# Score products of a two-layer diffusion trunk: two float32r products per head and block from stacked high and low parts

## The chip, the cores and the metric

The kernel runs on one core of a Trainium2 chip. The metric is the device time of one execution in microseconds, the median of several runs. A core has TensorE (matrix products), VectorE, ScalarE and GpSimd, which run side by side, each in the order of its own queue, and SyncE, which here only issues DMAs.

## The reference, cut to what matters

A trunk of two layers handles 128 prompt tokens and 256 sample tokens of width 1024. Each layer is a feed-forward part, a mixer and a second feed-forward part. The mixer of layer 0 (the even one) is a linear recurrence beside a differential attention; the mixer of layer 1 (the odd one) is a windowed attention with grouped queries. The sample tokens also see 128 cached keys.

```python
def diff_attn_block(qb, k, v, lam):              # even: 4 heads, each with 2 halves m of width 64
    s = jnp.einsum('bqhmd,bthmd->bhmqt', qb, k)
    p = jax.nn.softmax(s, axis=-1)
    w = p[:, :, 0] - lam * p[:, :, 1]
    return jnp.einsum('bhqt,bthe->bqhe', w, v)

def gqa_sink_block(qb, k, v, mask, sink):        # odd: 16 query heads of width 64 on 4 key heads
    s = jnp.einsum('bqkgd,btkd->bkgqt', qb, k)
    ...
```

Before these products queries and keys are normalized and, for the sample tokens, rotated. Everything is float32.

## The kernel before, in words

All data lie transposed: features on the 128 partitions (rows of a tile), the 384 tokens on the columns, 128 of the prompt and then 256 of the sample.

Weights come in chunks of 1 MB on SyncE's queue. Each group of eight 128x128 weights is split into a high part (a float32r copy, on ScalarE or VectorE) and a low part (a subtraction on VectorE), three groups ahead of their use. A weight product is then three float32r products (`mm3`): high with high, high with low, low with high.

The order of the work is made while the program is written. One main stream issues TensorE's projections (`proj_pass`, `out_pass`) and feed-forward products. All else runs as chains, Python generators that yield what they wait for. After each product `tick` looks at a list of chains and emits the stage whose inputs, by a table of estimated times, should be there. The recurrence of the even mixer (`lru_tile`) yields `DVE_IDLE` and `ACT_IDLE`: it is emitted where the engine is estimated to have nothing queued. The helper `copy` chooses between ScalarE and VectorE by the same estimates and takes VectorE only if that is done 0.5 us earlier. The estimates order the program and are not measurements.

In the even mixer the projection tiles are four for the recurrence, then query, key and value of each of four heads, then four gate tiles; then the output projection starts, with the K tiles of the four heads first and those of the recurrence last. In the odd mixer a key tile, a value tile and four query tiles come twice; each query tile holds two heads. There is no filler work in the odd mixer.

A query tile goes through `q_chain`: out of PSUM, norm, gain, a DMA that swaps the two rows of a rotary pair, two products and an add. A key tile goes through `k_chain`. A tile holds two score halves, rows 0 to 63 and 64 to 127, and the scores of each are needed alone. So `k_chain` writes each half into a tile of its own, `kz[0]` and `kz[1]`, whose other 64 rows GpSimd sets to zero, and beside it come the cached keys, stored with zeros in the same way. A product of the whole query tile with `kz[m]` then gives half m alone.

`scores` issues the products of one block: 128 queries (block 0 is the prompt, blocks 1 and 2 the sample) against 128 or 384 keys, for both m. In the even mixer a sample block is two fp32 products. In the odd mixer (`split=True`) query and keys are first split into high and low, and a sample block is six float32r products, three for each m, and then two mask products in bfloat16 (`identb`, `trib`). The prompt block is two fp32 products of 128 columns in both. The next step of a block (`a_chain`) is the softmax on VectorE and ScalarE, four or six transposes on TensorE, and `o_chain` applies the weights to the values.

PSUM has two banks for projections (`mm`), two pairs for scores (`sc`), which the feed-forward part uses too, and two for the rest (`ms`).

Of the kernel before, what the change touches and what calls it, by code (L numbers as in the profile page):

```python
# [15 lines left out]
ALU = mybir.AluOpType  # L16
# [13 lines left out]
RANGES = ((slice(0, NP_), 0), (slice(NP_, T), 1))  # L30
N_SLAB = 79
# [16 lines left out]
class Event:  # L48
    """Something that a chain of instructions has still to emit, with the tiles that it leaves."""
# [5 lines left out]
class Banks:  # L55
    """PSUM tiles of one tag: how many may be in use at a time, and when the free ones fell free."""
# [5 lines left out]
class Idle:  # L62
    """Ready when an engine has nothing else queued."""
# [19 lines left out]
class Clock:  # L83
    """Rough times of the engines while the program is written: they order the emission and nothing else."""
# [34 lines left out]
class Sched:  # L119
    """Emits the stages of side chains between pieces of the matmul stream, each when its inputs should be there."""  # L120
# [81 lines left out]
class Eng:  # L202
    """An engine's instructions, timed by the clock as they are written."""
# [50 lines left out]
def emit(tc, D, order):  # L254
    nc = tc.nc
    ctx = ExitStack()
    with ctx:
# [64 lines left out]
        def copy(out, in_, scale=None):  # L322
            """out = in_ (times a column), on the engine that should be done with it first."""
            k = {} if scale is None else {"scale": scale}
            r = max(clock.at(in_)[0], clock.at(out)[0])
            ta = max(clock.free["ACT"], r) + S_.cost("activation", out, [in_], k)
            td = max(clock.free["DVE"], r) + V.cost("tensor_copy", out, [in_] if scale is None else [in_, scale], k)
            if td + ON_ACT < ta:
                if scale is None:
                    V.tensor_copy(out, in_)  # L330
                else:
                    V.tensor_scalar(out, in_, scale, None, ALU.mult)
            else:
                act(out, in_, AF.Copy, **k)

# [140 lines left out]
        def mod_one():  # L476
            """Generator: one modulation tile, a condition per stage."""
# [44 lines left out]
        def prep(d, with_sh=True):  # L522
            """Generator: scaled x as two float32r parts, and the sum of squares."""
# [36 lines left out]
        def normed_all(low):  # L560
            """Starts the chains that leave the normed and modulated x as two float32r parts."""
# [152 lines left out]
        def qk_norm(t, bc, gate, gs):  # L714
            """Generator: leaves the normed rows in t, then returns the two parts of the rotated ones."""
# [29 lines left out]
        def q_chain(ps, direct, gate, gs, out):  # L745
            def gen():
# [5 lines left out]
                if not out.get("split"):  # L752
                    V.tensor_tensor(t[:, NP_:T], u[:, 0:NS], a[:, 0:NS], ALU.add)
                    sched.fire(out["q_ev"], t)
                    return
                V.tensor_tensor(u[:, 0:NS], u[:, 0:NS], a[:, 0:NS], ALU.add)
                hi, lo = sl(F32R, NS), sl(F32R, NS)
                yield u
                copy(hi, u[:, 0:NS])
                yield hi  # L760
                V.tensor_tensor(lo, u[:, 0:NS], r32(hi), ALU.subtract)
                out["qs"] = hi, lo
                sched.fire(out["q_ev"], t, hi, lo)
            sched.add(gen())

        def k_chain(ps, direct, gate, gs, out, ctx_src, k_out):
            def gen():
                yield ps
                t, bc = evac(ps, direct)
                kz = [sl(), sl()]  # L770
                kp = sl()
                kpv = kp.rearrange("p (a b) -> p a b", a=3)
                G.memset(kz[0][64:128, NP_:T], 0.0)
                G.memset(kz[1][0:64, NP_:T], 0.0)
                G.memset(kpv[64:128, 0, :], 0.0)
                G.memset(kpv[0:64, 1, :], 0.0)
                for m in range(2):
                    G.dma_start(kz[m][:, 0:NP_], ctx_src[m])
                out["kz"], out["kp"] = kz, kpv
                sched.fire(out["kp_ev"])  # L780
                yield t
                u, a = yield from qk_norm(t, bc, gate, gs["k"])
                for m in range(2):
                    h = slice(64 * m, 64 * m + 64)
                    V.tensor_tensor(kz[m][h, NP_:T], u[h, 0:NS], a[h, 0:NS], ALU.add)
                for m in range(2):
                    h = slice(64 * m, 64 * m + 64)
                    copy(kpv[h, m, :], t[h, 0:NP_])
                    G.dma_start(k_out[h, :], kpv[h, m, :])
                if not out.get("split"):  # L790
                    sched.fire(out["k_ev"], kz[0], kz[1], kp)
                    return
                out["ks"] = []
                for m in range(2):
                    hi, lo = sl(F32R), sl(F32R)
                    out["ks"].append((hi, lo))
                    yield kz[m]
                    copy(hi, kz[m])
                    yield hi
                    V.tensor_tensor(lo, kz[m], r32(hi), ALU.subtract)  # L800
                sched.fire(out["k_ev"], kp, *out["ks"][0], *out["ks"][1])
# [21 lines left out]
        def transposed(src, n):  # L823
            """w (128 queries, n*128 keys) -> SBUF (keys, n, queries)."""
# [8 lines left out]
        def scores(kv, q, qt, more=False):  # L833
            ps = sct()
            n = 1 if qt == 0 else 3
            for m in range(2):
                if qt and "ks" in kv:
                    (qh, ql), (kh, kl) = (v[:, (qt - 1) * P:qt * P] for v in q[1]), kv["ks"][m]
                    mm(ps[:, m, :n * P], qh, kh, True, False)
                    mm(ps[:, m, :n * P], ql, kh, False, False)  # L840
                    mm(ps[:, m, :n * P], qh, kl, False, not more)
                    continue
                rhs = kv["kp"][:, m, :] if qt == 0 else kv["kz"][m]
                mm(ps[:, m, :n * P], q[0][:, qt * P:(qt + 1) * P], rhs, True, not more)
            return ps, n

        def proj_pass(tiles, key, done, low):
            """Projection tiles in order; the first two share a K order that leaves the last tile of x late."""
# [32 lines left out]
        def out_pass(key, gm, nxt, ready, free_at, early, wide):  # L881
            """Output projection. The K tiles in `early` come first: x takes their part while the others are computed."""
# [8 lines left out]
            def slot(t, ps):  # L891
                """A bank that has nothing to do: kept while there are units to come."""
# [69 lines left out]
        def even_mixer(nxt):  # L962
# [136 lines left out]
            def a_chain(h, qt):  # L1099
                H = heads[h]  # L1100
                yield H["k_ev"], H["q_ev"], scb
                ps, n = scores(H, (H["q"], None), qt)
# [69 lines left out]
        def odd_mixer(nxt):  # L1172
# [6 lines left out]
            kvs = [dict(split=True, k_ev=Event(), v_ev=Event(), kp_ev=Event()) for _ in range(2)]  # L1179
            its = [dict(split=True, q_ev=Event(), w={}, w_ev=[Event() for _ in range(3)]) for _ in range(8)]  # L1180
# [69 lines left out]
        def mixer_consts():  # L1250
            yield RS.ev, el, pp
            # differential lambda, negated
# [5 lines left out]
            # -8 * softplus(-lam) on (128, 2 directions, 4 tiles); log1p by its series in z / (2 + z)  # L1258
# [91 lines left out]
# order of the 64 rows of a q or k head on the partitions: the two rows of a rotary pair side by side  # L1350
# [136 lines left out]
```

## Time and profile before

| | |
|---|---|
| median of 3 runs | 1466.14 us (1464.9 to 1466.73) |
| span of the profiled execution | 1464.2 us |
| instructions in the profile | 21823 |
| MB moved by DMA | 250.67 |
| even mixer | about 318 to 482 us of the span |
| odd mixer | about 1041 to 1188 us of the span |

The profiled execution's span runs from its first to its last instruction; it is the time that the profile tells of, and the runs' median lies 1.9 us above it. A busy share is the time in which an engine has at least one instruction in work. Nearly all instructions carry the line of one helper (L214), so groups are told apart by tile names: `sc`, `mm` and `ms` are the PSUM tiles, `s` is any tile of the general pool, `hi` and `lo` are the parts of a weight, `raw` a weight as it is loaded. An fp32 product appears as two records of TensorE, a float32r product as one. PEld is the loading of the stationary operand, which overlaps with products.

### The profile page before, as it was taken

Reading aid. Unit: us, or ns where it says so; the run is one execution under the profiler, and the core shown is the slowest. Engines: PE = TensorE matmul, PEld = TensorE weight load, DVE = VectorE, ACT = ScalarE, POOL = GpSimd, SP = SyncE. Lnnn points to the kernel's source line nnn. Section 1 sums busy time; section 2 is a strip of 40 time slices with the busy share of each in tenths; the row PEclk is TensorE's granted clock in tenths of the full one; section 3 lists DMA queues with packets and bytes.
Section 4 is the critical chain, followed back from the end, with each engine's and each line's share of the span. In section 5 each row is a group of like instructions: output and inputs, shape, how many; then the busy total and the mean of one; then the engine's idle time right before and its main releaser. Section 6 shows DMA issues by size and latency. Waiting matters only on the chain.

```text
span 1464.2 us, 21823 instructions
## 1 busy us (share of the span) xinstructions
PE 1436.7 (98%) x8354; PEld 1398.4 (96%) x8354; DVE 1115.4 (76%) x2103; ACT 659.8 (45%) x1193; POOL 103.8 (7%) x214
## 2 busy tenths in 40 slices
PE   4999999999999999999999999999999999999998
PEld 1999999998889999999999999999998899999998
DVE  3899999969998998999979997444698795444332
ACT  3643333348875633333345333333477664333321
POOL 0001111110220011111100110000100000000000
PEclk9999999999999999999999999999999999999999
DMA  9557767652322366766744766333331233333430
GB/s 361 216 185 257 246 245 257 235 173 101 120 99 97 140 230 236 254 243 231 254 177 153 251 243 196 135 119 130 117 107 51 77 120 115 133 126 116 146 135 22
DMA packets 49560, 250.67 MB, mean 171 GB/s; under 512 B 6464, under 2 KB 10960, under 8 KB 28336
## 3 DMA queue, kind: packets, MB, share of 16 engines
q1 hardware_dynamic: 29664, 180.05, 34.0%
q0 software_dynamic: 19792, 69.23, 14.2%
q8 instruction: 66, 1.08, 0.3%
q14 instruction: 38, 0.31, 0.1%
HBM read 244.53 MB, written 2.36 MB: 169 GB/s over the span
## 4 chain that ended last, share of the span: by engine, by line
PE 95%; DMA 2%; DVE 2%; ACT 1%; issue 0%; SPq 0%; DVEq 0%; ACTq 0%
PE sc L214 54%; PE mm L214 36%; PE ms L214 5%; DVE s L214 1%; DMA wm<-in_wm 1%; DMA s<-in_xT 1%; DMA raw<-in_wst 0%; DVE lo L214 0%; ACT s L214 0%; DMA s<-s 0%; ACT hi L214 0%; ACT L317 0%; SPq L737 0%; SPq L1296 0%; DVEq L1434 0%
## 5 line engine op out<-in xcount | busy, mean ns | idle before, releaser
L214 PE MATMUL sc<-s,hi 128*128 128x384 f32 (+1 forms) x2816 | 726.3, 339 | 2.3 <-ACT s L214 1.4
L214 ACT ACTIVATE hi<-raw 128x1024 fp32r<-128x1024 f32 x298 | 315.7, 1060 | 541.7 <-PE sc L214 307.4
L214 DVE TENSOR_TENSOR lo<-raw,hi 128x1024 fp32r<-128x1024 f32 x312 | 381.3, 1223 | 231.2 <-ACT hi L214 230.0
L214 PE MATMUL mm<-s,hi 128*128 128x384 f32 (+1 forms) x2072 | 545.8, 344 | 2.3 <-DVE s L214 2.3
L214 PEld LDWEIGHTS sc<-s,hi 128*128 128x128 f32 x2816 | 512.6, 188 | 5.0 <-ACT s L214 1.8
L214 PE MATMUL sc<-s,lo 128*128 128x384 f32 (+1 forms) x1408 | 475.4, 338 | 0.0
L214 PEld LDWEIGHTS mm<-s,hi 128*128 128x128 f32 x2072 | 372.9, 188 | 12.4 <-issue 3.0
L214 PE MATMUL mm<-s,lo 128*128 128x384 f32 (+1 forms) x1036 | 349.1, 337 | 0.0
L214 DVE CUSTOM_DVE_ANT_0 junk<-wm,cbc 128x1024 bf16<-128x1024 f32 x256 | 312.6, 1221 | 11.0 <-DMA wm<-in_wmt 8.3
L214 PEld LDWEIGHTS sc<-s,lo 128*128 128x128 f32 x1408 | 265.0, 188 | 0.0
L214 PEld LDWEIGHTS mm<-s,lo 128*128 128x128 f32 x1036 | 194.7, 188 | 0.0
L214 ACT ACTIVATE s<-s 128x384 f32<-128x384 f32 (+3 forms) x215 | 108.0, 507 | 171.9 <-DVE s L214 157.0
L214 DVE TENSOR_TENSOR s<-s,s 128x384 fp32r<-128x384 f32 (+6 forms) x214 | 112.0, 528 | 20.0 <-ACT s L214 18.9
L214 POOL DMA_DIRECT2D wm<-in_wmt x126 | 66.6, 528 | 695.1 <-DVE M L214 674.2
L214 DVE SCALAR_TENSOR_TENSOR s<-s,M,s 128x128 fp32r<-128x128 f32 (+3 forms) x256 | 92.4, 416 | 3.8 <-ACT s L214 3.7
L214 ACT ACTIVATE s<-s,M 128x256 fp32r<-128x256 f32 (+1 forms) x167 | 66.3, 446 | 11.0 <-DVE s L214 8.1
L214 DVE SCALAR_TENSOR_TENSOR s<-mm,M,s 128x128 f32<-128x128 f32 x104 | 38.5, 412 | 32.2 <-PE mm L214 32.2
L214 DVE TENSOR_TENSOR s<-sc,s 128x384 f32<-128x384 f32 x106 | 56.8, 551 | 0.0
L214 PE MATMUL sc<-s,s 128*128 128x384 f32 (+2 forms) x208 | 49.0, 373 | 0.7 <-ACT s L214 0.7
L214 ACT ACTIVATE s<-ms 128x384 f32<-128x384 f32 (+3 forms) x80 | 31.8, 423 | 29.8 <-PE ms L214 29.5
L214 PEld LDWEIGHTS sc<-s,s 128*128 128x128 f32 x208 | 34.1, 189 | 7.0 <-ACT s L214 1.3
L214 ACT ACTIVATE s<-sc,sm 128x385 f32<-128x385 f32 (+3 forms) x72 | 35.9, 511 | 0.0
(107 smaller groups left out, 635.1 us busy)
## 6 DMA issues: line engine op xcount, KB each, us to landing
raw<-in_wst SPq DMA_DIRECT2D x156, 1024.0 KB, 5.0
wm<-in_wmt POOLq DMA_DIRECT2D x126, 512.0 KB, 3.8
wm<-in_wm SPq DMA_DIRECT2D x8, 1024.0 KB, 7.6
s<-s SPq DMA_DIRECT2D x36, 64.0 KB, 2.4
s<-in_xT SPq DMA_DIRECT2D x8, 192.0 KB, 7.4
out_y<-s SPq DMA_DIRECT2D x8, 192.0 KB, 1.9
cbc<-in_c_rows SPq DMA_DIRECT2D x1, 1024.0 KB, 8.4
wm<-in_wmt SPq DMA_DIRECT2D x2, 512.0 KB, 9.7
```

The costliest lines, as they stand in the source:

```text
L214: r = fn(*a, **k)
```

## The change

A sample query tile is no longer split into a high and a low tile. Instead `q_chain` makes one tile per half m: the 64 rows of half m hold its high part, the other 64 rows hold its low part. The keys of half m are doubled: `k_chain` builds one tile `kk` with the cached and the new keys of both halves, and from it, per half m, a tile whose two row halves both hold the high part of that half's keys, and one whose row halves both hold the low part. One product of the stacked query with the doubled high keys sums (high + low) times high, a second with the doubled low keys sums (high + low) times low. So a sample block is two float32r products for each m, in both mixers. The zero-filled tiles `kz` and their memsets go, the cached keys are stored without zeros and loaded by one DMA instead of two, and the prompt block stays as it was. The comments in the source go too. Numbers that steer the order (`XN_E`, `O_EARLY` and the like) stay.

```diff
+HALF = (slice(0, 64), slice(64, 128))
...
                 u, a = yield from qk_norm(t, bc, gate, gs["q"])
                 out["q"] = t
-                if not out.get("split"):
-                    V.tensor_tensor(t[:, NP_:T], u[:, 0:NS], a[:, 0:NS], ALU.add)
-                    sched.fire(out["q_ev"], t)
-                    return
                 V.tensor_tensor(u[:, 0:NS], u[:, 0:NS], a[:, 0:NS], ALU.add)
-                hi, lo = sl(F32R, NS), sl(F32R, NS)
+                s = out["qs"] = [sl(F32R, NS), sl(F32R, NS)]
                 yield u
-                copy(hi, u[:, 0:NS])
-                yield hi
-                V.tensor_tensor(lo, u[:, 0:NS], r32(hi), ALU.subtract)
-                out["qs"] = hi, lo
-                sched.fire(out["q_ev"], t, hi, lo)
+                for m in range(2):
+                    copy(s[m][HALF[m], :], u[HALF[m], 0:NS])
+                for m in range(2):
+                    yield s[m]
+                    V.tensor_tensor(s[m][HALF[1 - m], :], u[HALF[m], 0:NS], r32(s[m][HALF[m], :]), ALU.subtract)
+                sched.fire(out["q_ev"], t, *s)
...
-                kz = [sl(), sl()]
+                kk = sl()
                 kp = sl()
                 kpv = kp.rearrange("p (a b) -> p a b", a=3)
-                G.memset(kz[0][64:128, NP_:T], 0.0)
-                G.memset(kz[1][0:64, NP_:T], 0.0)
                 G.memset(kpv[64:128, 0, :], 0.0)
                 G.memset(kpv[0:64, 1, :], 0.0)
-                for m in range(2):
-                    G.dma_start(kz[m][:, 0:NP_], ctx_src[m])
-                out["kz"], out["kp"] = kz, kpv
+                G.dma_start(kk[:, 0:NP_], ctx_src)
+                out["kp"] = kpv
...
+                V.tensor_tensor(kk[:, NP_:T], u[:, 0:NS], a[:, 0:NS], ALU.add)
                 for m in range(2):
-                    h = slice(64 * m, 64 * m + 64)
-                    V.tensor_tensor(kz[m][h, NP_:T], u[h, 0:NS], a[h, 0:NS], ALU.add)
+                    copy(kpv[HALF[m], m, :], t[HALF[m], 0:NP_])
+                    G.dma_start(k_out[HALF[m], :], kpv[HALF[m], m, :])
+                yield kk
+                ks = out["ks"] = [(sl(F32R), sl(F32R)) for _ in range(2)]
                 for m in range(2):
-                    h = slice(64 * m, 64 * m + 64)
-                    copy(kpv[h, m, :], t[h, 0:NP_])
-                    G.dma_start(k_out[h, :], kpv[h, m, :])
-                if not out.get("split"):
-                    sched.fire(out["k_ev"], kz[0], kz[1], kp)
-                    return
-                out["ks"] = []
+                    for h in HALF:
+                        copy(ks[m][0][h, :], kk[HALF[m], :])
                 for m in range(2):
-                    hi, lo = sl(F32R), sl(F32R)
-                    out["ks"].append((hi, lo))
-                    yield kz[m]
-                    copy(hi, kz[m])
+                    hi, lo = ks[m]
                     yield hi
-                    V.tensor_tensor(lo, kz[m], r32(hi), ALU.subtract)
-                sched.fire(out["k_ev"], kp, *out["ks"][0], *out["ks"][1])
+                    for h in HALF:
+                        V.tensor_tensor(lo[h, :], kk[HALF[m], :], r32(hi[HALF[m], :]), ALU.subtract)
+                sched.fire(out["k_ev"], kp, *ks[0], *ks[1])
...
-                if qt and "ks" in kv:
-                    (qh, ql), (kh, kl) = (v[:, (qt - 1) * P:qt * P] for v in q[1]), kv["ks"][m]
-                    mm(ps[:, m, :n * P], qh, kh, True, False)
-                    mm(ps[:, m, :n * P], ql, kh, False, False)
-                    mm(ps[:, m, :n * P], qh, kl, False, not more)
-                    continue
-                rhs = kv["kp"][:, m, :] if qt == 0 else kv["kz"][m]
-                mm(ps[:, m, :n * P], q[0][:, qt * P:(qt + 1) * P], rhs, True, not more)
+                if qt:
+                    qs, (kh, kl) = q[1][m][:, (qt - 1) * P:qt * P], kv["ks"][m]
+                    mm(ps[:, m, :n * P], qs, kh, True, False)
+                    mm(ps[:, m, :n * P], qs, kl, False, not more)
+                else:
+                    mm(ps[:, m, :n * P], q[0][:, 0:P], kv["kp"][:, m, :])
...
     dk = a["cache_diff_k"][0, 0].transpose(1, 2, 0)
-    dkz = np.zeros((4, 2, P, P), f)
-    dkz[:, 0, :64] = dk[:, ROPE]
-    dkz[:, 1, 64:] = dk[:, 64 + ROPE]
-    arr["dk"] = dkz
+    arr["dk"] = dk[:, np.concatenate([ROPE, 64 + ROPE])]
```

## Rows read from the trace of the kernel before

**Rows 1.** The page's first part: busy time, share of the span, instructions.

```profile
PE 1436.7 (98%) x8354; PEld 1398.4 (96%) x8354; DVE 1115.4 (76%) x2103; ACT 659.8 (45%) x1193; POOL 103.8 (7%) x214
```

**Rows 2.** The chain that ended last, by engine.

```profile
PE 95%; DMA 2%; DVE 2%; ACT 1%; issue 0%; SPq 0%; DVEq 0%; ACTq 0%
```

**Rows 3.** Windows: stretch, length, busy by engine, clock, DMA share, GB/s.

```profile
327.00:437.00 110.00, 109.68 (x587) 97.42 (x588) 105.78 (x239) 88.63 (x206) 21.69 (x49) 1.00 0.29 99
437.00:465.00 28.00, 28.00 (x166) 27.70 (x166) 23.17 (x49) 14.20 (x23) 0.00 (x0) 1.00 0.34 117
1061.00:1145.00 84.00, 83.75 (x625) 75.22 (x624) 77.97 (x210) 60.38 (x172) 2.28 (x4) 1.00 0.23 80
1145.00:1165.00 20.00, 19.27 (x157) 17.47 (x156) 12.92 (x33) 10.95 (x30) 0.00 (x0) 1.00 0.16 54
```

**Rows 4.** Waits of TensorE, 327 to 483 us: total, times, longest.

```profile
PE mm L214 <- DVE s L214: 2.0, 1, 2.0
PE sc L214 <- DVE s L214: 0.4, 1, 0.4
```

**Rows 5.** Waits of TensorE, 1047 to 1189 us.

```profile
PE sc L214 <- ACT s L214: 0.7, 1, 0.7
PE ms L214 <- ACT s L214: 0.6, 2, 0.4
```

**Rows 6.** Chain in order of time, even mixer: start, length, what, records.

```profile
391.81 1.29 PE sc L214 x4
393.10 2.63 PE mm L214 x15
```

**Rows 7.** Chain in order of time, odd mixer.

```profile
1091.47 1.06 PE mm L214 x6
1092.53 1.18 PE sc L214 x8
```

**Rows 8.** Groups by form, whole span: count, busy us, mean ns, idle before.

```profile
L214 DVE TENSOR_TENSOR s<-s,s 128x384 fp32r<-128x384 f32 x100 | 55.5, 555 | 14.8 <-ACT s L214 14.8
L214 ACT ACTIVATE s<-s 128x384 fp32r<-128x384 f32 x99 | 51.6, 523 | 105.9 <-DVE s L214 105.9
L214 PE MATMUL sc<-s,s 128*128 128x384 f32 x128 | 31.9, 381 | 0.7 <-ACT s L214 0.7
L214 DVE TENSOR_TENSOR s<-s,s 128x256 f32<-128x256 f32 x16 | 6.8, 424 | 0.4
L214 DVE TENSOR_TENSOR s<-s,s 64x256 f32<-64x256 f32 x12 | 5.0, 420 | 0.4
L214 POOL MEMSET s<- 64x256 f32 x12 | 3.7, 306 | 107.3 <-DVE s L214 106.9
L214 DVE TENSOR_TENSOR s<-s,s 128x256 fp32r<-128x256 f32 x8 | 3.4, 419 | 0.0
L214 ACT ACTIVATE s<-s 128x256 fp32r<-128x256 f32 x6 | 2.6, 430 | 0.0
L214 DVE CAST s<-s 128x384 fp32r<-128x384 f32 x1 | 0.4, 363 | 0.0
```

**Rows 9.** Groups of VectorE by form, 320 to 482 us.

```profile
L214 DVE TENSOR_TENSOR s<-s,s 128x387 f32<-128x387 f32 x20 | 11.0, 555 | 0.2
L214 DVE CAST hi<-raw 128x1024 fp32r<-128x1024 f32 x6 | 4.2, 692 | 0.6 <-PE mm L214 0.6
```

**Rows 10.** VectorE in order of time: start, length, what [idle before, releaser].

```profile
425.83 0.73 DVE L214 TENSOR_TENSOR_SCAN s<-s,pp,s 128x256 f32<-128x256 f32 x1
...
444.06 0.56 DVE L214 TENSOR_TENSOR s<-s,s 128x384 f32<-128x384 f32 x1 [1.73 <-ACT s L214]
...
446.46 0.55 DVE L214 TENSOR_TENSOR s<-s,s 128x384 fp32r<-128x384 f32 x1
...
459.40 0.56 DVE L214 TENSOR_TENSOR s<-s,s 128x384 fp32r<-128x384 f32 x1
...
465.47 0.74 DVE L214 SCALAR_TENSOR_TENSOR s<-mm,M,s 128x128 f32<-128x128 f32 x2 [1.29 <-PE mm L214]
```

More of the change, by code (lines that the diff above doesn't have):

```diff
@@ L1101, in a_chain @@
                 yield H["k_ev"], H["q_ev"], scb
-                ps, n = scores(H, (H["q"], None), qt)
+                ps, n = scores(H, (H["q"], H["qs"]), qt)
                 N = n * P
@@ L1178, in odd_mixer @@
             G.dma_start(sink, D["sink"].partition_broadcast(P))
-            kvs = [dict(split=True, k_ev=Event(), v_ev=Event(), kp_ev=Event()) for _ in range(2)]
-            its = [dict(split=True, q_ev=Event(), w={}, w_ev=[Event() for _ in range(3)]) for _ in range(8)]
+            kvs = [dict(k_ev=Event(), v_ev=Event(), kp_ev=Event()) for _ in range(2)]
+            its = [dict(q_ev=Event(), w={}, w_ev=[Event() for _ in range(3)]) for _ in range(8)]
             def a_chain(it, qt):
@@ L1408 @@
     dk = a["cache_diff_k"][0, 0].transpose(1, 2, 0)
-    dkz = np.zeros((4, 2, P, P), f)
-    dkz[:, 0, :64] = dk[:, ROPE]
-    dkz[:, 1, 64:] = dk[:, 64 + ROPE]
-    arr["dk"] = dkz
+    arr["dk"] = dk[:, np.concatenate([ROPE, 64 + ROPE])]
     arr["dv"] = a["cache_diff_v"][0, 0].transpose(1, 0, 2)
     wk = a["cache_win_k"][0, 0].transpose(1, 2, 0)
-    wkz = np.zeros((2, 2, P, P), f)
-    wkz[:, 0, :64] = wk[0::2][:, ROPE]
-    wkz[:, 1, 64:] = wk[1::2][:, ROPE]
-    arr["wk"] = wkz
+    arr["wk"] = np.concatenate([wk[0::2][:, ROPE], wk[1::2][:, ROPE]], axis=1)
     arr["wv"] = a["cache_win_v"][0, 0].reshape(P, 2, P).transpose(1, 0, 2)
```

## The prediction

> **What bounds the kernel now.** The page comes first. TensorE is busy for 98% of the span, VectorE for 76%, ScalarE for 45% [rows 1], and the chain that ended last lies on TensorE for 95% [rows 2]. So a microsecond of TensorE saved looks like a microsecond of time. But these are shares of the whole span, and all of the change sits in the two mixers. So next come windows over the stretches in which the attention runs. Even mixer: from 327 to 437 us VectorE is busy 105.78 of 110, from 437 to 465 it is busy 23.17 of 28. Odd mixer: from 1061 to 1145, 77.97 of 84, and then, to 1165, 12.92 of 20 [rows 3]. In both mixers two engines are nearly full at once. Which of them waits for the other? TensorE waits for VectorE 2.4 us in the whole even mixer [rows 4] and for ScalarE 1.3 us in the odd one [rows 5]. So TensorE sets the pace, and VectorE keeps up with 4% to 7% to spare. TensorE has its full clock (1.00, 2.4 GHz) in all of these stretches [rows 3].
>
> But part of VectorE's load can be moved: much of its even-mixer work is the recurrence (20 products of 387 columns alone are 11.0 us [rows 9]), which is emitted only when VectorE is estimated idle. The last scan ends at 426.6, and only then do idle gaps open (1.73 us at 444). The work of the last K tiles ends at 459.96, and at 465.47 VectorE waits 1.29 us for TensorE [rows 10]. So recurrence work may be pushed back by some microseconds, no more.
>
> **What the change removes on TensorE.** A sample block of the even mixer is two fp32 products of 384 columns, four records in 1.29 us; a float32r product beside it takes 2.63/15 = 0.175 us [rows 6]. Four float32r products replace them: 0.70 us. There are 4 heads x 2 blocks: 8 x 0.59 = 4.7 us. An odd block has six float32r products and two mask products, 1.18 us, at 1.06/6 = 0.177 us a weight product [rows 7]; two of the six go: 16 blocks x 0.35 = 5.6 us. The record count agrees: 128 records of that form are 16 fp32 products twice and 96 float32r ones [rows 8]. Sum 10.3 us, all on the path.
>
> **What it adds on VectorE and ScalarE.** Prices go by columns, not by rows: an add on 64 rows and 256 columns takes 0.420 us, one on 128 rows 0.424 [rows 8], so a half-tile instruction is charged in full.
> Even key: two 64-row adds become one 128-row add, and four subtractions of 384 columns come new: -0.84 + 0.42 + 4 x 0.555 = 1.80 us. Even query: two subtractions of 256 columns, 0.84 us. Four heads: 10.6 us of VectorE. The copies (four of 0.523 and two of 0.430 us on ScalarE) are 11.8 us of ScalarE [rows 8].
> Odd key: two subtractions become four, with the same saving on the add: 0.69 us; odd query: one more subtraction, 0.42. Two keys and eight queries: 4.8 us of VectorE; in the same way 5.5 us of ScalarE.
> The copy helper may put a copy on VectorE instead, at 0.363 us for 384 columns [rows 8].
>
> Half of the new subtractions of a key, both of a query, and half of the copies read one half of the rows and write the other. The trace has no such instruction. Below: the price of the same columns, as taken. Above: twice that, as if each half were passed on its own, some 8 us more of VectorE in each mixer. I take the lower end, since the 64-row rows show no dependence on which rows are used; the upper end goes into the last rival.
>
> On GpSimd the twelve 64x256 memsets of 0.306 us [rows 8] and six of the loads go. Nothing is priced for it: neither wait table has TensorE waiting for GpSimd [rows 4, 5]. One wait is new in its place: the first copy of an even key, on ScalarE, waits for the load of the cached keys, and the weight casts queue behind it. Before, only the products waited for that load. It is issued right after the projection is copied out of PSUM, a whole normalization and rotation ahead of the copy, so I price it at nothing; were it late, TensorE would feel it only after the three weight groups that are split ahead are used up.
>
> **Even mixer, summed.** From 327 to 465 VectorE did 128.95 us of work in 138. If TensorE saves its 4.7 us, the same stretch is 133.3 us long, and VectorE has 128.95 + 10.6 = 139.5 us to do. It doesn't fit. Two things help. The six weight casts that VectorE took over there, 4.2 us [rows 9], can go back to ScalarE, which is busy 102.8 of 138 and would be at 102.8 + 11.8 + 6.4 = 121; and the 9.05 us of idle time can be filled in part. I take all six casts away and a third of the idle time (3.0 us, waits for ScalarE as at 444) as left: 139.5 - 4.2 + 3.0 = 138.3, against 138 before: +0.3 us. The best end is -4.7 (VectorE finds all the room). The worst: no cast moves and half of the idle time stays, 139.5 + 4.5 = 144.0: +6.0. Behind 465 VectorE is booked solid with the updates of x, so what is late there stays late.
> The new latency of a key (four copies and four subtractions, some 3 us by the same prices) is covered for three heads by projections on TensorE. Next late is the fourth head: the output projection wants its K tile just after 446.46 + 0.55 = 447.0 [rows 10]; TensorE, if early, waits for it there. That is in the worst end.
>
> **Odd mixer, summed.** From 1061 to 1145: 77.97 + 4.8 = 82.8 us of VectorE in 84 - 5.6 = 78.4. Of the 6.0 us of idle time I leave 1.3, since VectorE would then nearly always have work in hand: 84.1, +0.1 us. Best end: the rest is done in the 7.1 idle us after 1145 and all of TensorE's gain stands, -5.6. Worst: half of the idle time stays (85.8), +1.8.
>
> Sum: 1464.2 + 0.3 + 0.1 = 1464.6 us of span. The profiled span lies 1.9 us below the median of the runs shown (1466.14), so the time is 1464.6 + 1.9 = 1466.5 us.
>
> **A rule weighed.** In the even mixer TensorE's weight loads are busy 97.42 of 110 us, VectorE 105.78 [rows 3]. The Trainium skill (Perfetto Trace Analysis, Identifying the Most-Contended Engine) judges TensorE by the busy share of its weight loads and VectorE by its occupancy, and calls the engine with the higher share the one to relieve. By that rule VectorE is the bottleneck of both mixers and the change loads the wrong engine; the last rival below is what it would make of the time. The trace agrees only in part: the shares stand so, but it was TensorE that had next to no waits.
>
> **Rivals.**
> 1. TensorE's gain stands in full, 1464.2 - 10.3 + 1.9 = 1455.8 us. For it: the chain, and waits of TensorE that are near nothing. Against it: the 139.5 us that don't fit into 133.3.
> 2. The odd mixer keeps its 5.6 us, since VectorE is free for 7.1 us just after the attention, and the even one breaks even: 1464.2 - 5.6 + 0.3 + 1.9 = 1460.8. For it: the odd mixer's load is the smaller one (4.8 us). Against it: the last queries' chain runs through just that slack.
> 3. VectorE becomes the bound of the even mixer. Recurrence work is pushed behind 447, the last K tiles of the output projection come late, TensorE waits at the late half: +6.0, with the odd mixer at +0.1: 1472.2. It decides from the point at which VectorE's unabsorbed load exceeds 4.7 us; for it speaks the 96% of 327 to 437, against it the casts that can move and the gaps behind 437.
> 4. Every added microsecond of VectorE lengthens its mixer: +10.6 + 4.8 = 15.4, 1481.5 us. It would need idle time that can't be used at all and copies that don't move, or the half-crossing instructions at double price. Against it: recurrence work that has been filler so far.
>
> **How the numbers follow.** Chances: forecast 0.37, rival 1 0.10, rival 2 0.24, rival 3 0.25, rival 4 0.04. A measurement of this kernel can't tell less than about 0.2%, 2.9 us, from no change: 1463.2 to 1469.1 counts as the same, and is the forecast's own range. Rivals 1 and 2 are faster: 0.34. Rivals 3 and 4 are slower: 0.29. The range 1457.5 to 1473.0 leaves out rival 1 but for its partial cases (0.08), rival 4 (0.04) and the upper part of rival 3 (0.06).
>
> **What would show it.** In the profile after: four score records of 384 columns per block in both mixers, 96 in all (8 x 4 + 16 x 4), a block at 0.70 us (even) and, with its masks, 0.83 us (odd). Subtractions of 64x384 at 0.55 and of 64x256 at 0.42 us, also across halves; if those that cross are dearer, rival 4's second leg holds. VectorE above 97% from the start of the even mixer's attention to the first late K tiles, casts of weights on VectorE fewer than six, TensorE's waits for VectorE or ScalarE in the mixers grown from 3.7 us to about 10: then the step "TensorE's gain is eaten by VectorE" is right. If the waits stay below 5 us and the mixers are shorter by 4.7 and 5.6 us, it is wrong and rival 1 holds. If TensorE waits over 12 us, rival 3.

## The result, and the profile after

The changed kernel takes 1479.64 us (median of four runs, 1477.87 to 1483.79), the kernel before beside it 1466.43: a ratio of 1.0094, 95% interval 1.0078 to 1.011, so 13.2 us slower. The forecast was 1466.5 with a range up to 1473.0: wrong. The profiled execution took 1483.79 us with a span of 1482.0, so it lies 4.2 us above the median; shares and orders below are read from it, the size of the loss is not.

The page's first part and its chain by engine, after:

```profile
PE 1442.7 (97%) x8322; PEld 1402.2 (95%) x8322; DVE 1134.5 (77%) x2141; ACT 673.3 (45%) x1221; POOL 97.0 (7%) x196
...
PE 87%; DVE 8%; DMA 2%; ACT 2%; issue 1%; SPq 0%; DVEq 0%; ACTq 0%
```

Against [rows 1, 2]: VectorE has 19.1 us more, ScalarE 13.5 more, and VectorE's part of the chain went from 2% to 8%. Which operations? Groups by form: PE over the whole span, VectorE from 328 to 500 us.

```profile
L215 PE MATMUL sc<-s,s 128*128 128x384 f32 x96 | 22.3, 354 | 1.0 <-ACT s L215 1.0
```

```profile
L215 DVE TENSOR_TENSOR s<-s,s 64x384 fp32r<-64x384 f32 x16 | 8.8, 551 | 0.2
L215 DVE CAST hi<-raw 128x1024 fp32r<-128x1024 f32 x7 | 4.8, 692 | 1.3 <-PE mm L215 1.3
L215 DVE TENSOR_TENSOR s<-s,s 64x256 fp32r<-64x256 f32 x8 | 3.4, 420 | 0.2
L215 DVE CAST s<-s 64x384 fp32r<-64x384 f32 x5 | 1.8, 355 | 0.1
L215 DVE CAST s<-s 64x256 fp32r<-64x256 f32 x3 | 0.8, 281 | 0.1
```

The 128 score records are 96, as forecast. The subtractions cost 0.551 and 0.420 us, those that cross the halves among them: no dearer. But the weight casts on VectorE are seven, not fewer than six [rows 9], and eight of the new copies joined them (2.6 us). The chain in order of time has a block at 0.70 us in the even mixer and at 0.83 in the odd one, both as forecast [rows 6, 7]:

```profile
379.55 0.70 PE sc L215 x4
...
1163.28 0.83 PE sc L215 x6
```

So the parts have the prices that were forecast, and the time went elsewhere. TensorE's waits, 327 to 500 us (total, times, longest), and three windows:

```profile
PE mm L215 <- DVE s L215: 8.2, 4, 3.3
PE mm L215 <- ACT s L215: 2.2, 2, 1.7
PE sc L215 <- DVE s L215: 1.7, 3, 1.1
PE ms L215 <- ACT s L215: 0.4, 1, 0.4
PE ms L215 <- DVE s L215: 0.2, 1, 0.2
```

```profile
328.00:438.00 110.00, 109.23 (x597) 100.47 (x598) 104.15 (x236) 91.70 (x213) 13.36 (x30) 0.98 0.29 99
438.00:466.00 28.00, 23.27 (x120) 22.04 (x119) 24.54 (x51) 14.60 (x27) 1.11 (x2) 0.88 0.26 98
466.00:500.00 34.00, 28.63 (x132) 26.28 (x131) 31.28 (x79) 18.29 (x41) 2.81 (x5) 0.83 0.18 66
```

TensorE waits 12.7 us where it waited 2.4 [rows 4]; 2.0 of it lie at the mixer's start in both, most of the rest behind 446 us (below, with the idle time before each). VectorE is busy for 95% up to 438, for 88% from there to 466 and for 92% from there to 500, not above 97%: it is loaded and still idles. The granted clock of TensorE falls to 0.88 and 0.83.

```profile
450.06 0.44 PE L215 MATMUL mm<-s,hi 128*128 128x384 f32 x1 [3.28 <-DVE s L215]
451.94 0.69 PE L215 MATMUL mm<-s,hi 128*128 128x384 f32 x1 [1.44 <-DVE s L215]
474.42 0.45 PE L215 MATMUL mm<-s,hi 128*128 128x384 f32 x1 [1.72 <-ACT s L215]
476.36 0.69 PE L215 MATMUL mm<-s,hi 128*128 128x384 f32 x1 [1.49 <-DVE s L215]
480.74 1.28 PE L215 MATMUL mm<-s,hi 128*128 128x384 f32 x2 [0.49 <-ACT s L215]
```

The first two wait for the fourth head's K tile, the others for tiles of the recurrence. VectorE in order of time shows why they are late:

```profile
449.92 3.50 DVE L215 TENSOR_TENSOR s<-s,s 128x384 f32<-128x384 f32 x9
...
457.79 0.74 DVE L215 SCALAR_TENSOR_TENSOR s<-ms,M,s 128x128 f32<-128x128 f32 x2 [0.99 <-PE ms L215]
460.09 0.74 DVE L215 SCALAR_TENSOR_TENSOR s<-ms,M,s 128x128 f32<-128x128 f32 x2 [1.56 <-PE ms L215]
...
477.15 0.73 DVE L215 TENSOR_TENSOR_SCAN s<-s,pp,s 128x256 f32<-128x256 f32 x1
...
480.72 0.56 DVE L215 TENSOR_TENSOR s<-s,s 128x384 fp32r<-128x384 f32 x1 [0.59 <-ACT s L215]
482.38 0.74 DVE L215 SCALAR_TENSOR_TENSOR s<-mm,M,s 128x128 f32<-128x128 f32 x2 [1.10 <-PE mm L215]
```

The last scan of the recurrence ends at 477.9 instead of 426.6 [rows 10]; the recurrence's last K tile is split at 480.72 instead of 459.40. Ahead of it stand updates of x (the tokens, to which the mixer's output is added), all of which come behind the last scan in the kernel before; and at 457.79 and 460.09 VectorE waits for TensorE while recurrence work is left over: it is in an order fixed beforehand.

To compare runs, take the even mixer from the end of TensorE's wait at its start to the end of its last wait for a tile of x in the second feed-forward. Windows of just that stretch, before and after:

```profile
327.32:481.89 154.57, 154.17 (x844) 141.12 (x844) 144.84 (x331) 116.47 (x264) 21.69 (x49) 1.00 0.30 105
```

```profile
328.21:499.30 171.09, 160.43 (x843) 148.05 (x843) 159.06 (x361) 124.39 (x279) 17.28 (x37) 0.94 0.27 93
```

VectorE's work grew by 14.2 us, its idle time (length less work) from 9.7 to 12.0. Of the work, 10.5 us are the subtractions less the saved adds, priced at 10.6; 2.6 are copies and 0.7 is the seventh cast. Every profile below is read in this way.

### The profile page after: what moved, and what is told of

It reads as the page before. It is cut to its first block, busy times and chain, and to the rows that moved or that the text cites. A ratio compares the mean times of both kernels' runs of the same rounds, so it can differ in the third digit from the quotient of the medians.

```text
span 1482.0 us, 21774 instructions
## 1 busy us (share of the span) xinstructions
PE 1442.7 (97%) x8322; PEld 1402.2 (95%) x8322; DVE 1134.5 (77%) x2141; ACT 673.3 (45%) x1221; POOL 97.0 (7%) x196
## 3 DMA queue, kind: packets, MB, share of 16 engines
q0 software_dynamic: 19600, 68.83, 14.1%
## 4 chain that ended last, share of the span: by engine, by line
PE 87%; DVE 8%; DMA 2%; ACT 2%; issue 1%; SPq 0%; DVEq 0%; ACTq 0%
PE sc L215 52%; PE mm L215 32%; DVE s L215 5%; PE ms L215 4%; DVE lo L215 1%; DMA wm<-in_wm 1%; ACT s L215 1%; DVE sm L215 1%; DMA s<-s 1%; DMA s<-in_xT 1%; ACT hi L215 0%; DVE sc L215 0%; ACT L318 0%; DVE hi L215 0%; DVEq L1417 0%
## 5 line engine op out<-in xcount | busy, mean ns | idle before, releaser
L215 PE MATMUL mm<-s,hi 128*128 128x384 f32 (+1 forms) x2072 | 548.2, 346 | 11.5 <-DVE s L215 8.5
L215 ACT ACTIVATE s<-s 128x384 f32<-128x384 f32 (+5 forms) x245 | 121.8, 502 | 176.1 <-DVE s L215 159.4
L215 DVE TENSOR_TENSOR s<-s,s 128x384 fp32r<-128x384 f32 (+5 forms) x244 | 126.7, 525 | 19.8 <-ACT s L215 17.8
L215 PE MATMUL sc<-s,s 128*128 128x384 f32 (+2 forms) x176 | 39.8, 358 | 1.0 <-ACT s L215 1.0
L215 PEld LDWEIGHTS sc<-s,s 128*128 128x128 f32 x176 | 28.7, 190 | 5.7 <-ACT s L215 2.1
```

What stands on the lines that cost most here:

```text
L215: r = fn(*a, **k)
```

## The experiments

All runs were timed beside the kernel before; the last column is the difference of the medians. The intervals of the ratios reach 1.4 to 3 us to either side, so two entries of that column within some 3 us of each other aren't told apart. Lengths are those of the even mixer in the one profiled execution, which for the changed kernel lies 4.2 us above its median. In e12 the even mixer is as before; its time stands in the text.

| run | VectorE's work | its idle time | length | TensorE busy | to before |
|---|---|---|---|---|---|
| before | 144.8 | 9.7 | 154.6 | 154.2 | |
| after | 159.1 | 12.0 | 171.1 | 160.4 | +13.2 |
| e1 odd only | 144.8 | 10.2 | 155.1 | 154.6 | +0.2 |
| e2 even only | 159.1 | 11.4 | 170.5 | 157.2 | +12.9 |
| e3 no low parts | 149.7 | 11.7 | 161.3 | 155.0 | +5.1 |
| e4 load on before | 155.4 | 10.0 | 165.4 | 158.1 | +10.7 |
| e5 before, GpSimd | 151.1 | 16.3 | 167.4 | 159.1 | +11.5 |
| e6 after, GpSimd | 161.1 | 12.9 | 174.0 | 158.9 | +17.3 |
| e7 no idle TensorE | 158.6 | 8.3 | 166.9 | 162.3 | +13.3 |
| e8 lean, GpSimd | 157.5 | 13.9 | 171.4 | 157.4 | +12.2 |
| e9 casts on ScalarE | 157.8 | 14.1 | 171.8 | 157.4 | +16.0 |
| e10 one low tile | 155.3 | 10.9 | 166.1 | 155.4 | +12.9 |
| e11 e9 and e10 | 153.7 | 15.6 | 169.3 | 155.5 | +17.0 |
| e13 order alone | 148.0 | 17.2 | 165.2 | 158.5 | +8.2 |
| e14 one head | 151.6 | 13.3 | 164.9 | 156.3 | +9.7 |
| e15 copies on ScalarE | 153.6 | 9.0 | 162.5 | 153.2 | +9.4 |
| e16 e10 and e15 | 151.0 | 11.9 | 162.9 | 153.7 | +9.0 |
| e17 recurrence first | 157.0 | 11.0 | 168.1 | 152.6 | +12.8 |
| e18 more banks | 153.6 | 13.0 | 166.7 | 153.5 | +14.8 |

**Which mixer: e1 and e2.** The change in one mixer alone, the other as before (its own functions, tables and key layout kept).

```
-                    q_chain(ps, direct, sig_done, gs, heads[j])
+                    q_chain_e(ps, direct, sig_done, gs, heads[j])
```

> The change in the odd mixer alone; the even mixer as before (two fp32 products per block, zero-padded keys). Theory A (the whole loss is the even mixer's: VectorE's added subtractions push the recurrence behind the attention, TensorE waits, and the waits bring its clock to 1.2 GHz): the time is that of the kernel before, 1466.4 within 2 us, and the granted clock is 1.00 in the even mixer. Theory B (both mixers pay, the odd one too, about a third by its share of the added work): 1470 to 1472. If the odd mixer keeps what TensorE saves there: 1460.8.

> The change in the even mixer alone; the odd mixer with its three float32r products as before. Theory A: 1479 to 1482, so all of the 13 us, with stretches of half clock between 450 and 503 us. Theory B: 1475 to 1476.

Odd only: ratio 1.0002 (0.9993 to 1.0012). Even only: 1.009 (1.0075 to 1.0105). The whole loss is the even mixer's; B falls, and A holds but for 0.6 us (1478.41, where it had 1479 at least). What became of the 5.6 us that the odd mixer should save on TensorE? Its waits in e1:

```profile
PE ms L215 <- ACT s L215: 1.9, 4, 0.7
PE sc L215 <- ACT s L215: 1.1, 1, 1.1
PE mm L215 <- ACT s L215: 0.7, 1, 0.7
PE ms L215 <- DVE s L215: 0.2, 1, 0.2
PE mm L215 <- DVE s L215: 0.2, 1, 0.2
```

That is 4.1 us against 1.3 [rows 5], most of it for ScalarE. TensorE's busy time in the same window (1047 to 1189) fell from 140.65 to 137.81 us, so by 2.8 us and not by 5.6, though there are 32 records fewer; why, no run shows. These 2.8 us are what the waits grew by. This stretch lost nothing and won nothing.

**Is it VectorE: e3 and e4.**

```
# e3, even mixer:
-    for h in HALF: V.tensor_tensor(lo[h, :], kk[HALF[m], :], r32(hi[HALF[m], :]), ALU.subtract)
+    ks[m] = (hi, hi)
-    V.tensor_tensor(s[m][HALF[1 - m], :], u[HALF[m], 0:NS], r32(s[m][HALF[m], :]), ALU.subtract)
+    G.tensor_copy(s[m][HALF[1 - m], :], u[HALF[m], 0:NS])
# e4, on the kernel before, per key and per query:
+    for m in range(3): V.tensor_tensor(d[0:64, :], t[0:64, :], t[0:64, :], ALU.subtract)
+    for m in range(2): V.tensor_tensor(d[0:64, 0:NS], u[0:64, 0:NS], a[0:64, 0:NS], ALU.subtract)
```

> The changed kernel, but the even mixer's new subtractions are not done on VectorE: the low part of a key is not computed (the high part is read in its place), and the other half of a query tile is a plain copy made by GpSimd. TensorE's products and ScalarE's copies are those of the changed kernel. Theory A (VectorE's added 10.6 us are the cause): the recurrence ends near 430 us again, TensorE's waits are as small as before, and TensorE's 4.7 us stand in part: 1461 to 1468. Theory C (the cause is the ScalarE copies, or the longer chain of a key before its first product, and VectorE's load is not): still above 1475.

> The kernel before, with subtractions of the same sizes added to the even mixer's keys (three of 64x384) and queries (two of 64x256) that nothing reads: 10.0 us more of VectorE, products and ScalarE copies as before. Theory A: the added work does the same harm without the new products: 1474 to 1482, with waits of TensorE of 3 us and more behind 440 us and a clock below 1.00 behind them. Theory C: 1466 to 1469, since the recurrence gives way and no key or query waits long.

e3, which leaves the low parts out, takes 1470.58, ratio 1.0035 (1.0021 to 1.0048): most of the loss goes with the subtractions, but 5.1 us stay, above A's range and below C's. VectorE still has 4.8 us more work than before, mostly copies that it took over; that these are the 5.1 us is argued, not shown. e4 takes 1476.22, ratio 1.0079 (1.0062 to 1.0096). Its even mixer:

```profile
327.11:492.47 165.36, 158.08 (x843) 142.91 (x843) 155.38 (x354) 116.25 (x262) 21.90 (x49) 0.98 0.29 98
```

10.5 us more work, 10.8 us more length, with no product and no ScalarE copy added: subtractions on VectorE suffice for a loss of this size, and C falls as the only cause. But the load doesn't come alone, since the planner orders the program anew around it. Of the 330 instructions that VectorE runs in the even mixer of the kernel before, all 330 stand in the same order in e1, 246 in e4 and 257 in e13 below, which changes the order on purpose (longest common sequence, by operation, shapes and tile names). No run adds the work and keeps the order.

**Other engines, and the clock: e5 to e8.** In e5 and e6 the planner's price for a GpSimd product and what the recurrence waits for change too, to match; in e8 GpSimd zeroes the other half of a key's low part.

```
# e5 (before) and e6 (after), recurrence:
-    V.tensor_tensor(li[dr, i], li[dr, i], xc[i], ALU.mult)
+    G.tensor_tensor(li[dr, i], li[dr, i], xc[i], ALU.mult)
-    V.tensor_tensor(u, u, li[dr, i], ALU.mult)
+    G.tensor_tensor(u, u, li[dr, i], ALU.mult)
# e7 (after), output projection, zz a tile of zeros:
+    if key == "e_out" and len(left) < len(ks):
+        while t > sched.now() + 0.6:
+            TE.matmul(ps[:, :T], lhsT=zz, rhs=ready[4][0], start=False, stop=False)
# e8 (after):
-    for h in HALF: V.tensor_tensor(lo[h, :], kk[HALF[m], :], r32(hi[HALF[m], :]), ALU.subtract)
+    h = HALF[m]; V.tensor_tensor(lo[h, :], kk[h, :], r32(hi[h, :]), ALU.subtract)
-    V.tensor_tensor(s[m][HALF[1 - m], :], u[HALF[m], 0:NS], ...)
+    G.tensor_tensor(s[m][HALF[1 - m], :], u[HALF[m], 0:NS], ...)
```

> The kernel before, with 16 products of 387 columns of the recurrence (two for each tile and direction, 8.9 us by VectorE's price) made on GpSimd instead of VectorE. Theory A2 (the length of the even mixer is VectorE's work plus some 10 us that can't be filled, once that sum is more than TensorE's work): before, both engines end together, TensorE is busy 156.5 of 157 us there, so relief of VectorE alone brings almost nothing: 1463 to 1467. Theory E (VectorE bounded the even mixer already before): 1458 to 1461. Had GpSimd's work slowed VectorE down through memory: above 1467.

> The changed kernel with the same 16 products on GpSimd. Theory A2: VectorE's work in the even mixer falls from 159.6 to about 150.7 us, and the time with it: 1470 to 1472. Theory F (what counts is the wait for the last head's K tile and the clock behind it, not the work): at most 3 us gained, 1476 or more.

> The changed kernel, with products of a zero weight tile (they add nothing to the sum) put into the output projection of the even mixer wherever its K tile is expected late, so that TensorE does not stand still there. Theory A2 (VectorE is the bound, so TensorE's clock hardly matters): 1477 to 1480, with the granted clock at 1.00 behind 446 us. Theory F (the stretches at 1.2 GHz, 24 us in all, cost up to half of their length): 1468 to 1474.

> The changed kernel with fewer subtractions on VectorE in both mixers: the low part of a key fills only its own half and the other half is zeroed by GpSimd (two subtractions of 64x384 for a key instead of four), and the low part of a query is subtracted by GpSimd. Products and copies are those of the changed kernel; the product of low part with low part falls away. VectorE's addition falls from 10.6 to 2.8 us in the even mixer and to less than nothing in the odd one. Theory A2: 1471 to 1473 from the even mixer, and 1 to 4 us less where the odd mixer can use it: 1467 to 1472. Theory F: above 1476, since the last head's chain of copies and subtractions is about as long as before, with GpSimd's slower subtractions in it.

e5 takes 1477.92 (1.0081, 1.0065 to 1.0097), e6 1483.69 (1.0112, 1.0094 to 1.013): products moved to GpSimd make the kernel before 11.5 us slower and the changed kernel no faster. That is the third case of e5's expectation; e6 lies in F's range, but with GpSimd in the way, as below. GpSimd takes 1.27 us in e5 for a product of 0.555 us on VectorE, and some of VectorE's instructions take much longer beside it. In e5, VectorE first, then GpSimd, in order of time:

```profile
365.59 2.71 DVE L214 SCALAR_TENSOR_TENSOR s<-s,sm,s 128x256 f32<-128x256 f32 x1
...
372.83 2.27 DVE L214 TENSOR_TENSOR s<-s,s 64x256 f32<-64x256 f32 x2
```

```profile
365.99 2.02 POOL L214 TENSOR_TENSOR s<-s,s 128x387 f32<-128x387 f32 x2
...
371.28 3.54 POOL L214 TENSOR_TENSOR s<-s,s 128x387 f32<-128x387 f32 x2
```

The first takes 0.48 us in the kernel before, each of the two 64x256 adds 0.42 [rows 8]. The Trainium skill (GPSIMD Engine Reference, Specifications) says that GpSimd shares its SBUF interfaces with VectorE and contends with its instructions of two SBUF inputs; the trace agrees for these, though not for every one: a weight's subtraction of 128x1024 that starts at 371.25, beside a GpSimd product, takes 1.21 us as elsewhere. So e5, e6 and e8 are no clean relief, and what they were to tell stays untold.

e7 takes 1479.67 (1.0088, 1.0068 to 1.0108). In its profile the granted clock is 1.00 throughout the even mixer, where the changed kernel had stretches at 0.50 (1.2 GHz):

```profile
452.00:458.00 6.00, 6.00 (x19) 6.00 (x20) 5.01 (x13) 1.99 (x3) 0.00 (x0) 0.50 0.01 1
476.00:485.00 9.00, 8.15 (x23) 7.34 (x24) 6.81 (x15) 1.90 (x6) 1.14 (x2) 0.50 0.00 0
```

```profile
327.57:494.52 166.95, 162.32 (x904) 150.94 (x904) 158.61 (x361) 124.26 (x279) 17.35 (x37) 1.00 0.28 95
```

The median is the same with and without them (1479.67 and 1479.64, by the intervals within some 4 us): F falls, and the fallen clock isn't what costs the 13 us. It may cost a part: this even mixer is 4.1 us shorter than the changed kernel's, but the two profiled executions differ by 4.5 us, and their medians don't. e8 takes 1478.59 (1.0084, 1.0069 to 1.01), outside A2's range and inside F's: of 7.8 us of subtractions taken away only 1.6 are missing from VectorE's work. The copy helper put five more 64x384 copies and three scalings of 128x384 out of PSUM on it, and some instructions grew longer (the 64x384 copies from 0.355 to 0.496 us).

**Does the amount alone decide: e9 to e12.**

```
# e9, e11: weight casts while the even mixer runs
-            copy(hi, r)
+            act(hi, r, AF.Copy)
# e10, e11, e12: one tile for the low parts
-                    for h in HALF:
-                        V.tensor_tensor(lo[h, :], kk[HALF[m], :], r32(hi[HALF[m], :]), ALU.subtract)
+                    V.tensor_tensor(kl[HALF[m], :], kk[HALF[m], :], r32(hi[HALF[m], :]), ALU.subtract)
```

> The changed kernel, with every weight cast of the even mixer put on ScalarE (the prediction assumed that six of them would go there; in the changed kernel seven stayed on VectorE). Theory A2 (length of the even mixer = VectorE's work plus about 10 us): 4.8 us off VectorE, 1474 to 1476. Theory G (ScalarE is as full as VectorE, and its chains set the end): 1478 or more, since 7 x 1.06 us come onto ScalarE.

> The changed kernel, in both mixers with one tile for the low parts of a key's two halves, each in its own half: two subtractions of 64x384 instead of four, nothing on GpSimd, queries as in the changed kernel. The second product of a row half takes the low part of its own half with the high part of the query; the other half of that tile meets the low part of the query only. VectorE has 4.4 us less in the even mixer than in the changed kernel. Theory A2: 1474 to 1476. Theory G: 1478 or more, since ScalarE's copies are the same.

> Both together: one tile for a key's low parts, and the weight casts of the even mixer on ScalarE. Theory A2: 9.2 us off VectorE, 1469 to 1472. Theory G: 1478 or more.

> The even mixer as before the change; in the odd mixer the change with one tile for a key's low parts. VectorE's addition in the odd mixer falls from 4.8 to 2.5 us by the prices of the prediction. Theory A2, if VectorE bounds the odd mixer too: 1462 to 1464, better than both kernels. Theory H (the odd mixer's chains through ScalarE are late, its waits are for ScalarE): 1465 to 1466, as with the change in the odd mixer alone.

1481.79 (1.0107, 1.009 to 1.0124), 1478.64 (1.0087, 1.0072 to 1.0102), 1482.78 (1.0114, 1.0099 to 1.0129), 1468.29 (1.0014, 1.0004 to 1.0023): A2 missed all four. Put the casts on ScalarE, as the prediction had assumed, and VectorE's work falls by 1.3 us only (other copies take their place) while its idle time rises to 14.1. e10 has 3.8 us less work on VectorE than the changed kernel, and its profiled even mixer is 5.0 us shorter; by medians it still loses 12.9 us. The same edit in the odd mixer ends at +2.5 us (e12), where the full change ended at +0.2 (e1), though VectorE has less to do; the intervals overlap, so that it is worse isn't shown, but that it is no better is. So the amount of VectorE's work alone doesn't set the time.

**Order, and how little it takes: e13 to e16.**

```
# e13, on the kernel before
-AHEAD = 0.6
+AHEAD = 0.45
# e14: the even mixer's change for head 0 only
+                    (q_chain if j < 1 else q_chain_e)(ps, direct, sig_done, gs, heads[j])
# e15 (after) and e16 (e10)
-ON_ACT = 0.5
+ON_ACT = 1.2
```

> The kernel before, all its work as it is; only the planner's constant AHEAD is 0.45 instead of 0.6, so that pieces of the recurrence are put behind attention work a little more often. Theory K (what decides is when the last K tile of the recurrence is ready for the output projection: up to about 465 us it costs nothing, later the second feed-forward starts 17 to 21 us behind it): the last recurrence tile comes at some 470 us, and the time is 1470 to 1474, though not one instruction is added. Theory A2 (VectorE's amount of work decides): 1465 to 1468.

> The change in the odd mixer and in the first of the four heads of the even one; the other three heads as before. VectorE's addition in the even mixer is a quarter, 2.65 us. Theory A2: a quarter of the 13 us at most, 1466 to 1469. Theory K: the first head's added work already shifts the order, the recurrence's last tile comes at 468 to 473 us, 1470 to 1475.

> The changed kernel, with the copy helper's constant ON_ACT at 1.2 instead of 0.5: more of the copies and casts stay on ScalarE, and with that the order changes. Theory K: the last recurrence tile is ready some 5 us earlier than in the changed kernel, and the time is 1474 to 1477. Theory G (ScalarE is as full as VectorE, as the run with all casts on it suggested): 1480 or more.

> The changed kernel with one tile for a key's low parts (two subtractions instead of four) and ON_ACT at 1.2. Theory K: the last recurrence tile at about 470 us and 1470 to 1475. Theory G: 1478 or more.

e13 takes 1474.19 (1.0058, 1.004 to 1.0076): 8.2 us from emission order alone. Its even mixer, and VectorE at the end of it:

```profile
327.17:492.41 165.24, 158.48 (x844) 143.48 (x844) 148.00 (x338) 115.10 (x257) 21.70 (x49) 0.98 0.29 98
```

```profile
464.54 0.74 DVE L214 SCALAR_TENSOR_TENSOR s<-ms,M,s 128x128 f32<-128x128 f32 x2 [0.49 <-PE ms L214]
...
469.70 1.23 DVE L214 TENSOR_TENSOR lo<-raw,hi 128x1024 fp32r<-128x1024 f32 x1 [1.54 <-ACT hi L214]
...
473.82 0.56 DVE L214 TENSOR_TENSOR s<-s,s 128x384 fp32r<-128x384 f32 x1 [0.59 <-ACT s L214]
```

Work +3.2 (five more copies out of PSUM on VectorE, which ScalarE made before), idle time 17.2 instead of 9.7, and the last recurrence tile at 473.82: the picture of the changed kernel without its work. e14 takes 1475.66 (1.0063, 1.0048 to 1.0078): a quarter of the change brings three quarters of the loss. Both end 0.2 and 0.7 us above K's ranges and far above A2's. e15 and e16 take 1475.43 (1.0069, 1.0049 to 1.0089) and 1474.98 (1.0061, 1.0045 to 1.0078): some 4 us better than the changed kernel, not worse; G falls, and both lie in K's ranges.

**Which link: e17 and e18.**

```
# e17 (after)
+            sched.ahead = 4.0
             out_pass("e_out", (0, 5), nxt, ready, ...)
+            sched.ahead = AHEAD
# e18 (after), output projection
+                if todo and key == "e_out" and ... and sched.when(scb) <= sched.now():
+                    ps = sct()
+                    for m in range(2):
+                        slot(sched.now(), ps[:, m, :])
```

> The changed kernel; from the start of the even mixer's output projection on, pieces of the recurrence are emitted ahead of other work of VectorE and ScalarE (the planner counts an engine as idle from 4.0 us ahead instead of 0.6). Theory K in its narrow form (the last recurrence tile alone decides): the tile is ready at some 465 us instead of 480.7, and the time is 1465 to 1470. Theory K2 (VectorE is full until the second feed-forward, so what comes earlier in the recurrence comes later in the last head and in the updates of x): no more than 3 us gained, 1476 to 1481, with the last head's K tile several us later.

> The changed kernel; the output projection of the even mixer borrows the four PSUM banks of the scores as well once the attention is done, so that all eight column tiles can take their products before the last recurrence tile comes. Theory K3 (the 17 to 21 us between the last recurrence tile and the second feed-forward are TensorE's late products, kept back by four banks): 6 to 9 us gained, 1470 to 1474. Theory K2 (they are VectorE's updates and preparations, busy 16.8 of 18.5 us there): no more than 3 us gained, 1476 to 1481.

1480.25 (1.0078, 1.0061 to 1.0095) and 1482.25 (1.0095, 1.008 to 1.011). In e17 the last recurrence tile is split 14 us earlier:

```profile
466.61 0.55 DVE L216 TENSOR_TENSOR s<-s,s 128x384 fp32r<-128x384 f32 x1
```

Yet the time is that of the changed kernel, and K in its narrow form falls: the last head's tile, split at 451.3 in the changed kernel, comes at 459.5, and TensorE waits there (7.2 us for its high part, 4.9 for its low part). In e18 the last recurrence tile is split at 482.66 and the even mixer ends 10.6 us behind it instead of 18.6, so the banks do what K3 had them do; but TensorE waits 3.5 us for tiles of x at the start of the feed-forward instead of 1.7, and nothing is gained, 1.3 us above K2's range even. In the other 17 profiles the mixer ends 17 to 23 us behind the last recurrence tile (22.5 before the change, 18.6 after): the lateness of that tile goes with the loss, but moving it, or what stands behind it, doesn't undo the loss. In these two orders the lateness went to another tile.

## Why the prediction was wrong

- **Prices: right.** Products, record counts, half-tile and half-crossing instructions, GpSimd at nothing: all as forecast.
- **Odd mixer, +0.1: right in size** (e1: +0.2, within 1.8 at most), **in part by luck.** TensorE's busy time fell by half of the 5.6 us. The prediction let VectorE's idle time be the limit. But what TensorE waits for there is ScalarE (3.7 of 4.1 us in e1), and with less work on VectorE the stretch got no faster (e12).
- **Even mixer, +0.3: the step that failed.** "I take all six casts away and a third of the idle time (3.0 us, waits for ScalarE as at 444) as left." Neither happened. A cast came to VectorE instead of six going, and eight copies with it: 14.2 us of added work for the forecast's 10.6 - 4.2 = 6.4. And the idle time hardly fell in any run: over 19 profiles it lies between 8.3 and 17.2 us of the even mixer, and the kernel before, at 9.7, was near the low end already. Work 14.2 and idle time 2.3 make the 16.5 us by which the profiled even mixer is longer; against the forecast (work +6.4, idle time from 9.05 to 3.0) it has 7.8 us more of work and 8.4 more of idle time. By medians the loss is 12.9 to 13.2 us; in the profile of the even-only kernel the mixer is 16.0 us longer, begins 1.6 us earlier, and 1.4 us are made up behind it: 13.0 us of span.
- **TensorE's 4.7 us** of savings are less than what its waits grew by, 10.3 us. The wait for the fourth head's K tile, which the prediction put "in the worst end", is 3.28 and 1.44 us of that, at 450 and 452.
- **Rival 3** had the mechanism (recurrence behind 447, late K tiles, TensorE's waits over 12 us: 12.7 in the even mixer) and a price of 6.0 that was half of what it cost. Its condition, unabsorbed load above 4.7 us, was met. **Rival 4** was nearest in time (1481.5) by another sum: odd 4.8 us that weren't lost, even 10.6 that were more. By the rule weighed there (the Trainium skill, Perfetto Trace Analysis, Identifying the Most-Contended Engine) VectorE was the bottleneck of both mixers. The runs bear it out for the even one, where subtractions added to VectorE cost 10.7 us (e4); in the odd one the order of the two shares turns round behind 1145 (weight loads 17.47 of 20 us, VectorE 12.92 [rows 3]), and e12 doesn't bear it out.
- **Missing altogether: the order.** The prediction took idle time as a reserve. It is set by an order that a planner writes from estimates, and e13 shows 7.5 us of it appearing with no work added to the program.

Shown: that the loss is the even mixer's (e1, e2), that subtractions added to VectorE there suffice without the new products and ScalarE copies (e4), that a new order with no work added costs 8.2 us (e13), that a clock held at 1.00 in that stretch gives nothing back that the medians show (e7). Open: how the 13 us divide into load and order, for e3, e4, e10 and e14 change both; and whether some order brings the changed kernel below 1466. None of the 18 runs did; the best, e1, equals the kernel before.

## What to carry to other kernels

Where two engines are both nearly full in a stretch (here 99.7% and 93.7%), an edit that shifts work from one to the other is to be priced as a loss of all that it adds, until a run shows that the receiving engine's idle time can be filled. Even that can be too little: e14 adds 2.65 us to the even mixer by its prices and costs 9.7. Idle time in a fixed emission order is waiting, not room. And where a planner orders the program, test what a small change of its constants does to the kernel before: if that alone moves the time by more than the gain sought, the forecast needs a range that holds it.

## What the runs showed of the hardware

Two things. Beside GpSimd products, an instruction of VectorE that takes 0.48 us in the kernel before took 2.71 (e5). And like waits of TensorE left TensorE's clock at full speed in one run and at half (1.2 GHz) for a while in another. At the even mixer's start TensorE waits about 2 us in both of these, having been busy for all of 300 to 320 us. The granted clock of the windows there is 1.00 and 0.86:

```profile
320.00:330.00 10.00, 8.01 (x44) 7.46 (x43) 7.56 (x29) 7.38 (x13) 0.00 (x0) 1.00 0.29 105
```

```profile
320.00:330.00 10.00, 8.01 (x38) 7.45 (x37) 7.52 (x28) 7.37 (x13) 0.00 (x0) 0.86 0.22 93
```

The first is the kernel before, the second e3; their edits differ only in work behind this stretch. What decided it, no run here shows.
